# Keys of both heads split at once and placed by transfers, with single sets of tiles, in a hybrid attention block

## The chip, the cores and the metric

The kernel runs on one core of a Trainium2 chip. The core's engines are named as the profile names them: PE multiplies matrices (PEld is its weight load), DVE is the vector engine, ACT the scalar engine with its function tables, POOL is GpSimd, and SP only issues transfers. The metric is the device time of one execution in microseconds; for each kernel several executions are timed and their median is given.

## The reference

The input is a sequence of 512 tokens of width 1024, with 16 learned tokens put in front (528 positions). After a layer norm, one matrix of 1024 x 10240 projects every position to ten groups of 1024 channels: queries, keys, values and gates of two attentions, and two merge gates. Both attentions work in causal blocks of 128 queries, so query block i (0 to 3) sees 16 + 128 (i + 1) keys: 144, 272, 400, 528.

```python
def diff_attn_block(q, k, v, q_pos, slopes, lam):          # 8 heads, each with 2 maps of width 64
    s = einsum(q, k) * 64 ** -0.5 ;  s = where(dist >= 0, s - slope * dist, -inf)
    p = softmax(s)
    a = p[map 0] - lam * p[map 1]
    return a @ v                                           # then an RMS norm per head

def stick_breaking_block(q, k, v, q_pos):                  # 16 heads of width 64
    before = k_pos < q_pos                                 # strictly earlier keys
    z = einsum(q, k) * 64 ** -0.5
    log_keep = where(before, log_sigmoid(-z), 0)
    suffix = cumsum of log_keep over the later keys
    a = where(before, exp(log_sigmoid(z) + suffix), 0)
    return a @ v
```

Each attention's output is multiplied with the SiLU of its gate and projected by a 1024 x 1024 matrix; the two results are merged by sigmoid gates, projected once more, added to the residual and normalised.

## The kernel before

All matrix products are done at reduced-precision speed with corrected operands: an operand is split into a rounded high part (a cast on ACT) and the remainder (a subtraction on DVE), and a product is the sum of high x high, high x low and low x high. Weights come in halves of 128 x 512 (`fetch`, L127), are split by `hi` (L153, ACT) and `lo` (L158, DVE) four halves ahead of their use, with six buffers of raw weights.

The work in the middle is a list of 16 units: eight differential heads ("d") and then eight pairs of stick-breaking heads ("s"). While the attention of unit u is computed, PE also projects the keys and values of unit u + 1 and the queries of unit u + 2; in "s" units two gates besides. `proj_tok` (L450 to L452) makes 512-wide products, `proj_pos` (L466) 264-wide ones, two halves of the 528 positions each.

- `stage_k` (L540) takes the projected keys of a unit from PSUM. Partitions 0 to 63 hold map or head 0, partitions 64 to 127 hold map or head 1. For each of the two, a tile `K[c]` of 128 x 2 x 528 is filled: its own half of the partitions with the high part and the remainder, the other half with the high part again and zeros (the queries' remainder stands there, so one product over 128 rows gives two of the three terms). The copies go from PSUM directly, for each c and each half: a cast (L551), a subtraction (L552) and a second cast to the other partitions (L553). There are two sets of `K`, used in turn.
- `logits` (L597) computes the scores of one query block: two products into one PSUM tile (high and low part of the keys, L608), except for block 0, whose 2 x 144 columns fit in one product (L602); there the low part's scores stand beside the high part's and are added on DVE (`with_lo`, L615). Block 3 (528 keys) is done in two halves.
- `d_scores` (L673): per query block from 3 down to 0 and per map, DVE adds the bias and finds the row's extreme (L701), ACT takes the exponential with its sum (L705); then DVE takes reciprocals (L709), multiplies one with -lambda (L710), scales the first map (L711) and combines both maps into `apad` (L712). The exponentials stand in tiles e0 and e1, two sets each.
- `s_scores` (L754): per query block DVE adds a mask of -1e30 to the last 128 columns of the scores (L767), ACT takes two sigmoids (`om` of -z, L770, and `sg` of z, L772), DVE multiplies `om` cumulatively from the last key backwards (a scan with a minimum that changes nothing, L775) and then `sg` with the shifted result into `apad` (L776).
- `transposed` (L618) turns `apad` on PE and splits it; `values` (L566) turns and splits the values; the products with them follow (`d_values`, `s_values`).

What sets the order: the first part up to L811 and the last from L848 are held to the written order by `keep_order`. In the middle each engine's order is set at build time by a planner, which simulates the engines and takes, of the instructions that are ready, the one written first. `run` (L495) writes the work down: the projections are a sequence of pieces with a nominal length, and attention's steps are put between them at due times (for a "d" unit: the ten score steps from 0.0 every 0.85, the three transposes from 11.0, the values' product at 14.5, out of 15.7 nominal). SP's queue, with all weight loads, and the other queues run in the planned order; an instruction whose semaphore is not there holds up all behind it on its queue.

Of the kernel before, what the change touches and what calls it, by code (L numbers as in the profile page):

```python
# [20 lines left out]
M = 16  # L21
L = M + S
NB = S // P
H2 = L // 2
# [7 lines left out]
ZW = 1344  # L32
# [11 lines left out]
def hybrid_block_kernel(ctx: ExitStack, tc: tile.TileContext, x, meta, emb_g, emb_b, w_in, b_gate,  # L44
# [209 lines left out]

    neg = const.tile([P, M + P], F32, name="neg")
    g.memset(neg, 0.0)
    g.affine_select(neg, neg, pattern=[[-1, M + P]], compare_op=ALU.is_gt, fill=-1e30, base=M, channel_multiplier=1)
# [249 lines left out]
    with tc.tile_pool(name="att", bufs=1) as ap:  # L507
# [7 lines left out]
        tails = {}  # L515
        for n in ("d", 0, 1):
            tails[n] = (ap.tile([P, P], F32R, name=f"v4{n}"), ap.tile([P, 32], F32R, name=f"a4{n}"))
            for t in tails[n]:
                g.memset(t.bitcast(F32), 0.0)


        keys = [[ap.tile([P, 2, L], F32R, name=f"k{c}{n}") for c in range(2)] for n in range(2)]
        for n in range(2):
            for c, oth in ((0, HI), (1, LO)):
                g.memset(keys[n][c][oth, 1, :].bitcast(F32), 0.0)  # L525
# [14 lines left out]
        def stage_k(unit, kind, n):  # L540

            pss = []
            proj = proj_pos(pss, "k" + kind, n)
            K = keys[n % 2]
            for m in range(2):
                while len(pss) == m:
                    yield next(proj, 0.33)
                o = ts(m, H2)
                for c, own, oth in ((0, LO, HI), (1, HI, LO)):
                    ps = pss[m][own, :H2]  # L550
                    s.copy(K[c][own, 0, o], ps)  # L551
                    v.tensor_tensor(K[c][own, 1, o], ps, K[c][own, 0, o].bitcast(F32), op=ALU.subtract)  # L552
                    s.copy(K[c][oth, 0, o], ps)  # L553
            unit["K"] = K

# [10 lines left out]
        def values(unit, kind):  # L566

            vT = unit["vT"]
            tv = ptp.tile([P, 512], F32, tag="tp", name="tv")
            for j in range(4):  # L570
                pe.transpose(tv[:, ts(j, P)], vT[:, ts(j, P)], ident)  # L571
            tvv = tv.rearrange("p (j d) -> p j d", j=4)
            V = [ap.tile([P, 4, P], F32R, tag=f"v{c}", name=f"V{c}") for c in range(2)]
            t4 = ptp.tile([P, 512], F32, tag="tp", name="t4")[:M, :P]
            pe.transpose(t4, vT[:, 512:528], ident)
            if kind == "d":
                s.copy(V[0][:, :3, :], tvv[:, :3, :])
                v.tensor_tensor(V[1][:, :3, :], tvv[:, :3, :], V[0][:, :3, :].bitcast(F32), op=ALU.subtract)
                vf = ap.tile([P, P], F32, tag="vf", name="vf")
                s.copy(vf, tvv[:, 3, :])  # L580
                v4 = tails["d"][0]
                s.copy(v4[:M], t4)
                s.copy(v4[32:32 + M], t4)
                v.tensor_tensor(v4[64:64 + M], t4, v4[:M].bitcast(F32), op=ALU.subtract)
                unit["V"] = V, vf
            else:
                for c, own, oth in ((0, LO, HI), (1, HI, LO)):
                    src = tvv[:, :, own]
                    s.copy(V[c][:, :, own], src)
                    v.tensor_tensor(V[c][:, :, oth], src, V[c][:, :, own].bitcast(F32), op=ALU.subtract)  # L590
                    v4 = tails[c][0]
                    s.copy(v4[:M, own], t4[:, own])
                    s.copy(v4[32:32 + M, own], t4[:, own])
                    v.tensor_tensor(v4[:M, oth], t4[:, own], v4[:M, own].bitcast(F32), op=ALU.subtract)
                unit["V"] = V

        def logits(A, K, i):  # L597

            nk, q = NKEY[i], A[:, ts(i, P)]
            if 2 * nk <= 512:  # L600
                ps = psc.tile([P, 512], F32, tag="sc", name="sc")
                pe.matmul(ps[:, :2 * nk].rearrange("p (a n) -> p a n", a=2), q, K[:, :, :nk], start=True, stop=True)  # L602
                yield ps, 0, nk, ps[:, nk:2 * nk]
                return
            for k0, n in [(0, nk)] if nk <= 512 else [(0, H2), (H2, H2)]:
                ps = psc.tile([P, 512], F32, tag="sc", name="sc")
                for m in range(2):
                    pe.matmul(ps[:, :n], q, K[:, m, k0:k0 + n], start=(m == 0), stop=(m == 1))  # L608
                yield ps, k0, n, None

        def with_lo(lo, b, t):

            if lo is None:
                return b
            v.tensor_tensor(t, lo, b, op=ALU.add)  # L615
            return t
# [56 lines left out]
        def d_scores(unit, h):  # L673

            K = unit["K"]
# [11 lines left out]
            E = [ap.tile([P, ZW], F32, tag=f"e{c}", name=f"e{c}", bufs=2) for c in range(2)]  # L687
# [3 lines left out]
            for i in reversed(range(NB)):  # L691
                nk = NKEY[i]
                e = [E[c][:, ZOFF[i]:ZOFF[i] + nk] for c in range(2)]
                for c in range(2):
                    m = mn[:, i, c, :]
                    for n, (ps, k0, use, lo) in enumerate(logits(A[c], K[c], i)):
                        if n == 1:
                            yield
                        b0 = 384 - P * i + k0
                        t = with_lo(lo, bias[:, b0:b0 + use], e[c][:, k0:k0 + use])  # L700
                        v.tensor_tensor_reduce(e[c][:, k0:k0 + use], ps[:, :use], t, -1.0, 3e38, ALU.add, ALU.min,  # L701
                                               m[:, n:n + 1])
# [7 lines left out]
                v.tensor_scalar(r[:, 1:2], r[:, 1:2], nlam, None, op0=ALU.mult)  # L710
                v.tensor_scalar(e[0], e[0], r[:, 0:1], None, op0=ALU.mult)  # L711
# [42 lines left out]
        def s_scores(unit, c, first):  # L754
            K = unit["K"]
            A = unit["A"]
            a = apads[c]
            sg = ap.tile([P, ZW], F32, tag="e0", name="sgm", bufs=2)
            om = ap.tile([P, ZW], F32, tag="e1", name="om", bufs=2)
            for i in reversed(range(NB)):  # L760
                nk, z0 = NKEY[i], ZOFF[i]
                for n, (ps, k0, use, lo) in enumerate(logits(A[c], K[c], i)):
                    if n == 1:
                        yield
                    if k0 + use == nk:
                        w = P if lo is None else use
                        v.tensor_tensor(ps[:, use - w:use], ps[:, use - w:use], with_lo(lo, neg[:, M + P - w:], om[:, ds(z0, w)]),  # L767
                                        op=ALU.add)
# [36 lines left out]
        run([stage_k(units[0], *UNITS[0])], [(2.7, then)])  # L805
# [7 lines left out]
        for u, (kind, n) in enumerate(UNITS):  # L813
# [6 lines left out]
            pending = []  # L820
            if kind == "d":
# [256 lines left out]
```

## Time and profile before

| | before |
|---|---|
| median of 3 runs (range) | 732.13 us (731.3 to 732.39) |
| the profiled execution, its own time | 732.59 us |
| its span from first to last instruction | 730.8 us |
| mean granted clock of PE | 0.995 |
| busy: PE, DVE, ACT, POOL | 718.3, 580.3, 447.2, 89.9 us |
| bytes moved by transfers | 71.84 MB |

A page of the profile lists busy times, the chain of work that ended last, and groups of instructions by line with their shape, count, busy time and mean duration in ns, and the idle time of the engine before them. The waits view lists who waited for whom: total us, times, longest. A timeline row has start, duration (of the whole row, if several like instructions are merged), engine, line, operation, output and inputs, shape and count. A row of the windows view has a stretch, its length, and for PE, PEld, DVE, ACT and POOL the busy time with the count of rows, then the granted clock, the transfer engines' share and GB/s. Transfers have size and median time from issue to landing. Matmul durations overlap: one starts before the one ahead has ended.

### The profile page before, as it was taken

The numbers are of one execution on the slowest core, as the hardware profiler recorded it, in microseconds if no ns is written. First come the engines' busy times: TensorE is split into PE (matmuls) and PEld (weight loads), VectorE is DVE, ScalarE is ACT, GpSimd is POOL, SyncE is SP. The second block draws the span as 40 slices with busy tenths as digits, with TensorE's granted clock in tenths as the row PEclk, the third lists the DMA queues.
The fourth block names the chain that finished last, engine by engine and source line by source line (L and its number), as shares of the span: only waits on it lengthen the run. The fifth ranks groups of instructions, "written<-read, shape, count | busy, mean of one in ns | idle before, by whom it ended". The sixth has DMA issues, their size and how long they took to land.

```text
span 730.8 us, 13070 instructions
## 1 busy us (share of the span) xinstructions
PE 718.3 (98%) x4658; PEld 657.6 (90%) x4658; DVE 580.3 (79%) x1304; ACT 447.2 (61%) x1101; POOL 89.9 (12%) x116
## 2 busy tenths in 40 slices
PE   9999999999999999999999999999999999999994
PEld 8999999999999989898989898988888998999883
DVE  6888778878886699696969696969476888788887
ACT  5686677777877858575757574756355456555300
POOL 3211110011000000000000000001012202130002
PEclk9999999999999999999999999999999999999998
DMA  9142221222132221323132212222239837696902
GB/s 280 50 116 87 60 73 44 87 59 73 45 87 58 73 73 53 92 61 86 45 90 70 85 46 87 73 73 59 73 89 181 177 105 185 135 183 188 315 16 102
DMA packets 121347, 71.84 MB, mean 98 GB/s; under 512 B 4241, under 2 KB 114994, under 8 KB 121282
## 3 DMA queue, kind: packets, MB, share of 16 engines
q1 hardware_dynamic: 111650, 64.18, 30.0%
q0 software_dynamic: 9312, 5.77, 6.0%
q10 hardware_dynamic: 320, 1.06, 0.4%
q8 instruction: 37, 0.61, 0.3%
q14 instruction: 28, 0.23, 0.1%
HBM read 67.32 MB, written 2.10 MB: 95 GB/s over the span
## 4 chain that ended last, share of the span: by engine, by line
PE 89%; DVE 5%; DMA 3%; POOL 1%; ACT 1%; issue 1%; SPq 0%; POOLq 0%; DVEq 0%; ACTq 0%
PE ps L466 25%; PE ps L450 12%; PE ps L451 12%; PE ps L452 12%; PE q L886 10%; PE sc L608 5%; PE t L621 4%; DMA raw<-in_w_out_dram 2%; PE t L626 1%; PE bank L341 1%; PE av L789 1%; PE tv L571 1%; PE av L790 1%; DMA eb<-in_emb_ln_b_dram 1%; DVE hr L1035 1%
## 5 line engine op out<-in xcount | busy, mean ns | idle before, releaser
L158 DVE TENSOR_TENSOR wl<-raw,wh 128x512 fp32r<-128x512 f32 x180 | 124.3, 697 | 47.8 <-ACT wh L153 46.7
L466 PE MATMUL ps<-hTh,wh 128*128 128x264 f32 x512 | 147.4, 288 | 0.0
L466 PE MATMUL ps<-hTl,wh 128*128 128x264 f32 x512 | 146.3, 286 | 0.0
L466 PE MATMUL ps<-hTh,wl 128*128 128x264 f32 x512 | 145.8, 285 | 0.0
L452 PE MATMUL ps<-hTh,wl 128*128 128x512 f32 x368 | 144.8, 393 | 0.0
L450 PE MATMUL ps<-hTh,wh 128*128 128x512 f32 x368 | 144.7, 393 | 0.0
L451 PE MATMUL ps<-hTl,wh 128*128 128x512 f32 x368 | 144.5, 393 | 0.0
L153 ACT CAST wh<-raw 128x512 fp32r<-128x512 f32 x180 | 109.9, 621 | 49.8 <-PE ps L451 38.9
L466 PEld LDWEIGHTS ps<-hTh,wh 128*128 128x128 f32 x512 | 96.4, 188 | 1.2
L466 PEld LDWEIGHTS ps<-hTl,wh 128*128 128x128 f32 x512 | 96.4, 188 | 0.7
L466 PEld LDWEIGHTS ps<-hTh,wl 128*128 128x128 f32 x512 | 96.4, 188 | 0.3
L452 PEld LDWEIGHTS ps<-hTh,wl 128*128 128x128 f32 x368 | 69.2, 188 | 13.5
L451 PEld LDWEIGHTS ps<-hTl,wh 128*128 128x128 f32 x368 | 69.2, 188 | 12.9
L450 PEld LDWEIGHTS ps<-hTh,wh 128*128 128x128 f32 x368 | 69.2, 188 | 12.7
L886 PE MATMUL q<-gh,wh 128*128 128x256 f32 x224 | 63.5, 283 | 0.2 <-ACT t L895 0.2
L886 PE MATMUL q<-gh,wl 128*128 128x256 f32 x224 | 63.4, 283 | 0.0
L886 PE MATMUL q<-gl,wh 128*128 128x256 f32 x224 | 63.4, 283 | 0.0
L632 DVE TENSOR_TENSOR al<-t,ah 128x512 fp32r<-128x512 f32 (+2 forms) x88 | 45.7, 526 | 17.9 <-ACT ah L631 11.0
L775 DVE TENSOR_TENSOR_SCAN om<-om 128x528 f32<-128x528 f32 (+1 forms) x64 | 55.7, 877 | 5.1 <-ACT om L770 4.4
L608 PE MATMUL sc<-k,A 128*128 128x264 f32 (+2 forms) x256 | 56.4, 308 | 0.2 <-POOL k L525 0.2
L631 ACT CAST ah<-t 128x512 fp32r<-128x512 f32 (+2 forms) x88 | 40.0, 465 | 25.4 <-PE t L621 18.1
L770 ACT ACTIVATE om<-sc 128x264 f32<-128x264 f32 (+3 forms) x80 | 31.8, 397 | 20.0 <-DVE sc L767 17.7
(243 smaller groups left out, 1442.3 us busy)
## 6 DMA issues: line engine op xcount, KB each, us to landing
raw<-in_w_in_dram SPq DMA_DIRECT2D x152, 256.0 KB, 3.0
raw<-in_w_out_dram SPq DMA_DIRECT2D x16, 256.0 KB, 3.6
raw<-in_w_br_diff_dram SPq DMA_DIRECT2D x12, 256.0 KB, 4.3
raw<-in_w_br_sb_dram SPq DMA_DIRECT2D x12, 256.0 KB, 4.5
raw<-in_w_in_dram SPq DMA_DIRECT2D x4, 512.0 KB, 6.2
rawa<-in_w_br_diff_dram SPq DMA_DIRECT2D x8, 256.0 KB, 4.6
rawa<-in_w_br_diff_dram POOLq DMA_DIRECT2D x8, 256.0 KB, 5.9
rawa<-in_w_br_sb_dram SPq DMA_DIRECT2D x8, 256.0 KB, 4.1
```

The source lines that it names most:

```text
L153: s.copy(wh, raw)
L158: eng.tensor_tensor(wl, raw, wh.bitcast(F32), op=ALU.subtract)
L450: pe.matmul(ps, wh[:, k % 4, :], hTh[:, k, M:], start=(k == 0), stop=False)
L451: pe.matmul(ps, wh[:, k % 4, :], hTl[:, k, M:], start=False, stop=False)
L452: pe.matmul(ps, wl[:, k % 4, :], hTh[:, k, M:], start=False, stop=(k == KT - 1))
L466: pe.matmul(ps[:, :H2], a[:, k % 4, :], b[:, k, ts(c, H2)], start=(k == 0 and m == 0), stop=(k == KT - 1 and m == 2))
L608: pe.matmul(ps[:, :n], q, K[:, m, k0:k0 + n], start=(m == 0), stop=(m == 1))
L631: s.copy(h, t[:, o:o + w])
L632: v.tensor_tensor(l, t[:, o:o + w], h.bitcast(F32), op=ALU.subtract)
L770: s.activation(om[:, o], ps[:, :use], AF.Sigmoid, scale=-1.0)
L775: v.tensor_tensor_scan(rev, rev, rev, 1.0, ALU.mult, ALU.min)
L886: pe.matmul(bank, a[:, k, :], b[:, n, k, :], start=start and k == 0 and m == 0, stop=k == 3 and m == 2, skip_group_check=not start)
```

## The change

- Keys: `stage_k` now splits both heads at once. One cast and one subtraction over all 128 partitions write a staging tile `t` (two of them, one per half). A new function `store_k` copies from it into the four places of `K[0]` and `K[1]` by transfers on SP's queue, eight per unit. There is one set of `K`. `store_k` is put among the steps of the unit before at 9.2 nominal (10.6 in the first "s" unit). Unit 0 keeps the direct copies (`direct=True`).
- Scores: the form of block 0 with both parts in one product goes; block 0 is done like blocks 1 and 2, with two products into the same columns. `with_lo` goes.
- Exponentials: one set of e0 and e1 (`E`) for all units, and the two sigmoids of `s_scores` stand in them too.
- Mask: the tile `neg` and the addition to the scores go. The scan's second input is a tile `after` (1 at masked keys, 0 elsewhere) with a maximum, so that it stays at 1 through the masked keys; GpSimd sets the masked part of `sg` to zero.
- First map: its scaling and the product of the reciprocal with -lambda move from DVE to GpSimd.
- Values of the "s" units: the copies for both heads are done by one instruction each, through strided views of one tile `V`, and likewise for the last 16 positions (`v4s`).

```diff
-    neg = const.tile([P, M + P], F32, name="neg")
-    g.memset(neg, 0.0)
-    g.affine_select(neg, neg, pattern=[[-1, M + P]], compare_op=ALU.is_gt, fill=-1e30, base=M, channel_multiplier=1)
...
+        v4d = ap.tile([P, P], F32R, name="v4d")
+        v4s = ap.tile([P, 4, 64], F32R, name="v4s")
...
+        E = [ap.tile([P, ZW], F32, name=f"e{c}") for c in range(2)]
+        after, staged = [], []
...
-        keys = [[ap.tile([P, 2, L], F32R, name=f"k{c}{n}") for c in range(2)] for n in range(2)]
-        for n in range(2):
-            for c, oth in ((0, HI), (1, LO)):
-                g.memset(keys[n][c][oth, 1, :].bitcast(F32), 0.0)
+        K = [ap.tile([P, 2, L], F32R, name=f"k{c}") for c in range(2)]
+        for c, own, oth in HEADS:
+            g.memset(K[c][oth, 1, :].bitcast(F32), 0.0)
...
-        def stage_k(unit, kind, n):
+        def stage_k(unit, kind, n, direct=False):
...
-                o = ts(m, H2)
-                for c, own, oth in ((0, LO, HI), (1, HI, LO)):
-                    ps = pss[m][own, :H2]
-                    s.copy(K[c][own, 0, o], ps)
-                    v.tensor_tensor(K[c][own, 1, o], ps, K[c][own, 0, o].bitcast(F32), op=ALU.subtract)
-                    s.copy(K[c][oth, 0, o], ps)
-            unit["K"] = K
+                o, ps = ts(m, H2), pss[m][:, :H2]
+                if direct:
...
+                t = ap.tile([P, 2, H2], F32R, tag="ks", name="ks", bufs=2)
+                s.copy(t[:, 0], ps)
+                v.tensor_tensor(t[:, 1], ps, t[:, 0].bitcast(F32), op=ALU.subtract)
+                staged.append((o, t))
+
+        def store_k():
+
+            for o, t in staged:
+                for c, own, oth in HEADS:
+                    nc.sync.dma_start(K[c][own, :, o].bitcast(F32), t[own].bitcast(F32))
+                    nc.sync.dma_start(K[c][oth, 0, o].bitcast(F32), t[own, 0].bitcast(F32))
+            staged.clear()
...
-                for c, own, oth in ((0, LO, HI), (1, HI, LO)):
-                    src = tvv[:, :, own]
-                    s.copy(V[c][:, :, own], src)
-                    v.tensor_tensor(V[c][:, :, oth], src, V[c][:, :, own].bitcast(F32), op=ALU.subtract)
...
+                for h, l, src in ((V[:, :, 0:4:3], V[:, :, 1:3], tvv.rearrange("p j (c d) -> p j c d", c=2)),
+                                  (v4s[:M, 0:4:3], v4s[:M, 1:3], t4.rearrange("p (c d) -> p c d", c=2))):
+                    s.copy(h, src)
+                    v.tensor_tensor(l, src, h.bitcast(F32), op=ALU.subtract)
...
-            if 2 * nk <= 512:
-                ps = psc.tile([P, 512], F32, tag="sc", name="sc")
-                pe.matmul(ps[:, :2 * nk].rearrange("p (a n) -> p a n", a=2), q, K[:, :, :nk], start=True, stop=True)
-                yield ps, 0, nk, ps[:, nk:2 * nk]
-                return
...
-            E = [ap.tile([P, ZW], F32, tag=f"e{c}", name=f"e{c}", bufs=2) for c in range(2)]
...
-                v.tensor_scalar(r[:, 1:2], r[:, 1:2], nlam, None, op0=ALU.mult)
-                v.tensor_scalar(e[0], e[0], r[:, 0:1], None, op0=ALU.mult)
+                g.tensor_scalar(e[0], e[0], r[:, 0:1], None, op0=ALU.mult)
+                g.tensor_tensor(r[:, 1:2], r[:, 1:2], nlam, op=ALU.mult)
...
-            sg = ap.tile([P, ZW], F32, tag="e0", name="sgm", bufs=2)
-            om = ap.tile([P, ZW], F32, tag="e1", name="om", bufs=2)
+            sg, om = E
...
-                    if k0 + use == nk:
-                        w = P if lo is None else use
-                        v.tensor_tensor(ps[:, use - w:use], ps[:, use - w:use], with_lo(lo, neg[:, M + P - w:], om[:, ds(z0, w)]),
-                                        op=ALU.add)
...
+                own = sg[:, ds(z0 + nk - P, P)]
+                g.affine_select(own, own, pattern=[[-1, P]], compare_op=ALU.is_gt, fill=0.0, base=0, channel_multiplier=1)
                 rev = om[:, z0:z0 + nk][:, ::-1]
-                v.tensor_tensor_scan(rev, rev, rev, 1.0, ALU.mult, ALU.min)
+                v.tensor_tensor_scan(rev, rev, after[0][:, L - nk:][:, ::-1], 1.0, ALU.mult, ALU.max)
...
-        run([stage_k(units[0], *UNITS[0])], [(2.7, then)])
+        run([stage_k(units[0], *UNITS[0], True)], [(2.7, then)])
...
+            if not last:
+                steps.append((10.6 if kind == 's' and n == 0 else 9.2, store_k))
...
+                    after.append(ap.tile([P, L], F32, tag="bias", name="after", bufs=2))
+                    g.memset(after[0], 0.0)
+                    own = after[0][:, L - P:]
+                    g.affine_select(own, own, pattern=[[-1, P]], compare_op=ALU.is_gt, fill=1.0, base=0, channel_multiplier=1)
```

More of the change, by code (lines that the diff above doesn't have):

```diff
@@ L515, in hybrid_block_kernel @@
         tails = {}
+        v4d = ap.tile([P, P], F32R, name="v4d")
+        v4s = ap.tile([P, 4, 64], F32R, name="v4s")
         for n in ("d", 0, 1):
-            tails[n] = (ap.tile([P, P], F32R, name=f"v4{n}"), ap.tile([P, 32], F32R, name=f"a4{n}"))
-            for t in tails[n]:
-                g.memset(t.bitcast(F32), 0.0)
-        keys = [[ap.tile([P, 2, L], F32R, name=f"k{c}{n}") for c in range(2)] for n in range(2)]
-        for n in range(2):
-            for c, oth in ((0, HI), (1, LO)):
-                g.memset(keys[n][c][oth, 1, :].bitcast(F32), 0.0)
+            tails[n] = (v4d if n == "d" else v4s[:, 2 * n:2 * n + 2].rearrange("p c d -> p (c d)"),
+                        ap.tile([P, 32], F32R, name=f"a4{n}"))
+        for t in (v4d, v4s, *(tails[n][1] for n in tails)):
+            g.memset(t.bitcast(F32), 0.0)
+        E = [ap.tile([P, ZW], F32, name=f"e{c}") for c in range(2)]
[3 more added lines that the diff above has]
+            g.memset(K[c][oth, 1, :].bitcast(F32), 0.0)
         def stage_q(unit, kind, n):
@@ L572, in values @@
             tvv = tv.rearrange("p (j d) -> p j d", j=4)
-            V = [ap.tile([P, 4, P], F32R, tag=f"v{c}", name=f"V{c}") for c in range(2)]
+            V = ap.tile([P, 1024], F32R, tag="v", name="V")
             t4 = ptp.tile([P, 512], F32, tag="tp", name="t4")[:M, :P]
@@ L576, in values @@
             if kind == "d":
+                V = V.rearrange("p (c j d) -> p c j d", c=2, j=4)
+                V = [V[:, c] for c in range(2)]
                 s.copy(V[0][:, :3, :], tvv[:, :3, :])
@@ L586, in values @@
             else:
-                for c, own, oth in ((0, LO, HI), (1, HI, LO)):
-                    src = tvv[:, :, own]
-                    s.copy(V[c][:, :, own], src)
-                    v.tensor_tensor(V[c][:, :, oth], src, V[c][:, :, own].bitcast(F32), op=ALU.subtract)
[L591 to L595, printed above, removed]
+                V = V.rearrange("p (j c d) -> p j c d", j=4, c=4)
+                for h, l, src in ((V[:, :, 0:4:3], V[:, :, 1:3], tvv.rearrange("p j (c d) -> p j c d", c=2)),
+                                  (v4s[:M, 0:4:3], v4s[:M, 1:3], t4.rearrange("p (c d) -> p c d", c=2))):
+                    s.copy(h, src)
+                    v.tensor_tensor(l, src, h.bitcast(F32), op=ALU.subtract)
+                s.copy(v4s[32:32 + M, 0:4:3], t4.rearrange("p (c d) -> p c d", c=2))
+                unit["V"] = [V[:, :, 2 * c:2 * c + 2].rearrange("p j c d -> p j (c d)") for c in range(2)]
         def logits(A, K, i):
             nk, q = NKEY[i], A[:, ts(i, P)]
-            if 2 * nk <= 512:
-                ps = psc.tile([P, 512], F32, tag="sc", name="sc")
-                pe.matmul(ps[:, :2 * nk].rearrange("p (a n) -> p a n", a=2), q, K[:, :, :nk], start=True, stop=True)
-                yield ps, 0, nk, ps[:, nk:2 * nk]
-                return
             for k0, n in [(0, nk)] if nk <= 512 else [(0, H2), (H2, H2)]:
@@ L608, in logits @@
                     pe.matmul(ps[:, :n], q, K[:, m, k0:k0 + n], start=(m == 0), stop=(m == 1))
[L609 to L616, printed above, removed]
+                yield ps, k0, n
         def transposed(ta, a, head):
@@ L673, in d_scores @@
         def d_scores(unit, h):
-            K = unit["K"]
             A = unit["A"]
@@ L695, in d_scores @@
                     m = mn[:, i, c, :]
-                    for n, (ps, k0, use, lo) in enumerate(logits(A[c], K[c], i)):
+                    for n, (ps, k0, use) in enumerate(logits(A[c], K[c], i)):
                         if n == 1:
```

14 lines of the change are left out of this document (8 added, 6 removed).

## The prediction, made before the changed kernel ran

> **What bounds the kernel now.** I read the page first: busy time and the chain that ended last.
>
> ```profile
> span 730.8 us, 13070 instructions
> PE 718.3 (98%) x4658; PEld 657.6 (90%) x4658; DVE 580.3 (79%) x1304; ACT 447.2 (61%) x1101; POOL 89.9 (12%) x116
> PE 89%; DVE 5%; DMA 3%; POOL 1%; ACT 1%; issue 1%; SPq 0%; POOLq 0%; DVEq 0%; ACTq 0%
> ```
>
> PE is busy 98% of the span and holds 89% of the chain. A busy PE may still be a badly fed one, so the second view is what PE waited for, and the third its share between the first scores of one head and of the next, and in one pair of stick-breaking heads.
>
> ```profile
> PE sc L608 <- POOL k L525: 0.2, 1, 0.2
> PE q L886 <- ACT t L895: 0.2, 1, 0.2
> ...
> 132.21:156.42 24.21, 24.21 (x174) 22.90 (x172) 20.62 (x60) 18.33 (x49) 3.23 (x2) 1.00 0.23 67
> 156.42:180.62 24.20, 24.20 (x174) 22.87 (x172) 19.40 (x60) 18.26 (x49) 3.12 (x2) 1.00 0.20 58
> ...
> 415.00:452.00 37.00, 37.00 (x238) 33.59 (x237) 29.76 (x61) 23.29 (x62) 2.58 (x2) 1.00 0.25 72
> ```
>
> After its warm-up PE waits 0.4 us in all. In both kinds of unit (24.2 us per differential head, 37.0 us per stick-breaking pair) it is busy throughout at the full granted clock, while DVE is busy 19.4 to 20.6 of 24.2 us and 29.8 of 37. Work taken from DVE and ACT therefore buys nothing here; work added to PE is paid in full. The question that decides is what the change adds to PE, and PE's own durations overlap, so I take prices from the spacing of starts in the timeline.
>
> ```profile
> 296.54 0.39 PE L452 MATMUL ps<-hTh,wl 128*128 128x512 f32 x1
> 296.77 0.24 PE L789 MATMUL av<-ah,V 128*128 128x160 f32 x1
> 296.84 0.43 PE L450 MATMUL ps<-hTh,wh 128*128 128x512 f32 x1
> 297.11 0.40 PE L451 MATMUL ps<-hTl,wh 128*128 128x512 f32 x1
> ...
> 173.31 0.29 PE L602 MATMUL sc<-k,A 128*128 128x288 f32 x1
> 173.44 0.28 PE L466 MATMUL ps<-hTh,wh 128*128 128x264 f32 x1
> ...
> 156.54 0.27 PE L621 MATMUL t<-idents,apad 128*128 128x128 f32 x1
> 156.54 0.60 PE L621 MATMUL t<-idents,apad 128*128 128x128 f32 x4
> ...
> L602 PE MATMUL sc<-k,A 128*128 128x288 f32 x32 | 9.7, 304 | 0.0
> ```
>
> A 512-wide product takes 0.23 us (296.54 to 296.77). A 160-wide one seems to take 0.07, but the 512 behind it then takes 0.27: the pair costs 0.34, so the narrow one costs 0.34 - 0.23 = 0.11. One 128-wide transpose lasts 0.27 and four in a row span 0.60 (two answers on the same stretch), so they start (0.60 - 0.27) / 3 = 0.11 apart. A product narrower than 264 columns thus has a floor near 0.11 us. The 288-wide score product of query block 0 costs 0.13 (173.31 to 173.44).
>
> **The change part by part.** *Scores of query block 0 (L600 to L604).* One product over both parts of the keys, 288 wide, becomes two of 144, each with its own weight load (the page counts 4658 of either). 32 products (the L602 row: 16 units, 2 maps) become 64. By the floor: 2 x 0.11 to 0.12 - 0.13 = 0.09 to 0.11, times 32 = 2.9 to 3.5 us. If only the visible spacing counted (0.07): 2 x 0.07 - 0.13 = 0.01, times 32 = 0.3 us. I take 0.115: 0.10 x 32 = 3.2 us, since the floor shows twice, in a transpose and in a narrow product.
>
> The Trainium skill ("TensorE: Matmul & The Clock Gate", section Back-to-back issue gap) gives about 81 ns per product for a stream of weight loads and products at 128 columns; taken as it stands for 144 columns, that is an estimate of 2 x 0.081 - 0.13 = 0.03, or 1.0 us over 32 pairs. The 0.11 us of this trace at 128 and 160 columns speaks against it, and the measurement decides.
>
> *Work that leaves DVE and ACT.*
>
> ```profile
> L552 DVE TENSOR_TENSOR k<-ps,k 64x264 fp32r<-64x264 f32 x64 | 27.3, 427 | 8.2 <-ACT k L551 7.3
> L553 ACT CAST k<-ps 64x264 fp32r<-64x264 f32 x64 | 24.0, 374 | 15.1 <-DVE k L552 14.2
> L563 ACT COPY vT<-ps 128x264 f32<-128x264 f32 x32 | 12.2, 381 | 0.3
> L767 DVE TENSOR_TENSOR sc<-sc,neg 128x128 f32<-128x128 f32 x48 | 13.7, 289 | 1.9 <-PE sc L608 1.3
> L767 DVE TENSOR_TENSOR sc<-sc,om 128x144 f32<-128x144 f32 x16 | 4.9, 308 | 0.3
> L615 DVE TENSOR_TENSOR e<-sc,bias 128x144 f32<-128x144 f32 x16 | 4.8, 301 | 0.1
> L710 DVE TENSOR_SCALAR rz<-rz,nlam 128x1 f32<-128x1 f32 x32 | 6.8, 211 | 0.8
> L711 DVE TENSOR_SCALAR e<-e,rz 128x528 f32<-128x528 f32 x8 | 3.9, 485 | 0.0
> L711 DVE TENSOR_SCALAR e<-e,rz 128x272 f32<-128x272 f32 x8 | 2.9, 362 | 0.0
> ```
>
> Partitions do not set a duration (64x264 takes 374 ns on ACT, 128x264 takes 381), so both heads at once halve it. Keys: DVE 4 x 0.427 to 2, saving 0.85 us a unit; ACT eight of 0.374 to two of 0.381, saving 2.2. A differential head also loses L710 (4 x 0.211), L711 (0.485, 0.362 and two between or just below: about 1.55) and L615 (2 x 0.301): DVE saves 3.8 us of some 20. A stick-breaking pair loses the mask (6 x 0.289 + 2 x 0.308) and its two L615 forms (0.6): with the keys 3.8 us of 29.8; the merged copies of values save a few tenths more. In all about 60 us of DVE and 35 of ACT, priced at nothing: they lie beside a PE that never waits. At most the 0.2 us of L608 could return.
>
> *Work that goes to POOL.*
>
> ```profile
> L684 POOL TENSOR_SCALAR bias<-bias 128x528 f32<-128x528 f32 x8 | 14.1, 1758 | 21.8 <-DVE e L615 21.6
> L257 POOL TENSOR_SCALAR_AFFINE_SELECT neg<-neg 128x144 f32<-128x144 f32 x1 | 0.3, 298 | 0.0
> 148.60 1.40 POOL L735 TENSOR_TENSOR sql<-sq,sqh 128x512 fp32r<-128x512 f32 x1 [18.32 <-ACT sqh L734]
> 148.88 1.42 DVE L712 SCALAR_TENSOR_TENSOR apad<-e,rz,e 128x272 f32<-128x272 f32 x1
> 152.71 0.37 DVE L712 SCALAR_TENSOR_TENSOR apad<-e,rz,e 128x144 f32<-128x144 f32 x1
> ```
>
> Scaling the first map is the operation of L684: 1.76 us for 528 columns, by width 1.33, 0.91 and 0.48 for the others, 4.5 us a head, plus four tiny products. L712 now queues on DVE behind that. The last one of this head ends at 153.1 and its first transposes start at 156.54: 3.4 us of cover, against 0.48 us for the last block, or 1.4 with the block before still running. Without cover it would be about 1 us a head, 8 us. The selection on the sigmoid (8 a pair, about 0.3 us each) runs beside the scan over the other tile. DVE and POOL do disturb each other: L712 took 1.42 us beside L735. The Trainium skill ("SBUF — State Buffer", section Who interferes with whom) calls this an exclusive lock between a DVE instruction with two SBUF inputs and a GpSimd one that reads SBUF; the row agrees. Even if all 4.5 us fell on DVE, a head's DVE would be at 20.6 - 3.8 + 4.5 = 21.3 of 24.2: still under PE.
>
> *Keys by transfers, one set.*
>
> ```profile
> 174.63 0.29 PE L602 MATMUL sc<-k,A 128*128 128x288 f32 x1
> 180.62 0.65 PE L608 MATMUL sc<-k,A 128*128 128x264 f32 x4
> 175.16 0.37 SPq L127 DMA_DIRECT2D raw<-in_w_in_dram  x1
> raw<-in_w_in_dram SPq DMA_DIRECT2D x152, 256.0 KB, 3.0
> out_dram<-hr SPq DMA_DIRECT2D x8, 256.0 KB, 2.0
> ```
>
> Eight transfers a unit, 120 in all, of at most 132 KB, are queued on SP among the weight loads. They wait for the last scores (ended 174.9 here), because the one set is still read until then; the next scores start at 180.62, 5.7 us later. Eight issues of 0.37 are 3.0 us, and landing takes 2.0 to 3.0 (a transfer between two tiles is not in this trace): the last lands 5.0 to 6.0 us after the last scores. The first scores need only one map's four, the second map's follow them. So it is hidden, barely. Weight loads queued behind wait up to 3 us more, with six buffers ahead: nothing. In stick-breaking units the gates stand between and the window is wider.
>
> *First unit.*
>
> ```profile
> 32.85 0.28 PE L608 MATMUL sc<-k,A 128*128 128x264 f32 x1
> 33.34 0.39 PE L608 MATMUL sc<-k,A 128*128 128x264 f32 x1 [0.20 <-POOL k L525]
> ```
>
> Here PE waits for POOL clearing the keys; half of that clearing goes: 0 to -0.4 us, I take -0.2.
>
> **The sum.** 3.2 - 0.2 = +3.0 us on PE's chain. The profiled execution took 732.59 us (span 730.8 and 1.8 around it), 0.46 above the median of 732.13; so 735.6 for such an execution, 735.1 against the median.
>
> **The rivals.** *A, narrow products are cheap (ends on the other side):* two adjacent products on the same weights might run at the visible 0.07 us spacing, the debt being paid only once. For it: the 0.07 itself. Against: the 0.27 behind it, and each 144 has its own load. It decides where the pair costs below 0.18 us; price +0.3 - 0.2: 732.2, no change. *B, the relief returns time:* a lighter DVE lets the planner place PE's work better. For it: DVE ends late behind the projections, so scores are spread out. Against: two equal heads take 24.21 and 24.20 us, both wholly busy. Removing all the 0.4 us of waits beside rival A gives 731.9; to be faster than noise it needs some 1.5 us that no row shows: 730.4. *C, keys come late:* if the scores stand ahead of the landing, or one load (0.37) sits among the eight, the last lands at 174.9 + 6.0 + 0.4 = 181.3, 0.7 late, at eight boundaries between differential heads and into the first pairs: +5.6 us, 740.7. For it: the 5.7 us window. Against: half the transfers suffice to start, and the planner has projections to put in between. It decides when landing exceeds the window.
>
> **How the numbers follow.** Forecast 0.52; A 0.15; B 0.16, of which 0.09 faster; C 0.17. Below 0.2% (1.5 us, about what a measurement tells from no change) counts as the same. Slower: 0.52 + 0.17 = 0.69; same 0.15 + 0.07 = 0.22; faster 0.09. The forecast's own range is 734.5 to 735.8. The range 732.0 to 739.5 takes in A, most of B and the milder half of C, and leaves out under 2 in 10.
>
> **What the new profile would show.** Right: the L602 form is gone, 64 products of 144 columns stand in its place, pair spacing near 0.22 us; PE still about 98% with no wait on the keys; DVE near 520 us, ACT near 410, POOL near 150; heads 24.4 instead of 24.2 us apart. Wrong: pair spacing near 0.14 (A); PE's waits naming a transfer into the keys (C); a shorter distance between heads with PE's count up (B). A first transpose that waits for the probabilities would break the cover given to POOL.

## The result and the profile after

| | before | changed |
|---|---|---|
| median (range), 5 runs each | 732.13 us (731.26 to 732.39) | 736.03 us (734.92 to 737.56) |
| ratio, 95% interval | | 1.006 (1.0044 to 1.0077) |
| the profiled execution, its own time | 732.59 us | 734.92 us |
| its span | 730.8 us | 733.1 us |
| bytes moved by transfers | 71.84 MB | 84.03 MB |

The changed kernel is slower, by 3.9 us in the medians; the forecast was +3.0 us, 735.1. The two profiled executions differ by 2.3 us, in time and in span alike. First the page of the changed kernel: its span, its busy times, its chain by engine, and two of its transfer groups (count, size, median us from issue to landing).

```profile
span 733.1 us, 13328 instructions
PE 719.2 (98%) x4690; PEld 659.4 (90%) x4690; DVE 529.9 (72%) x1098; ACT 411.1 (56%) x987; POOL 176.6 (24%) x241
PE 88%; DVE 6%; DMA 3%; POOL 1%; issue 1%; ACT 1%; SPq 0%; POOLq 0%; ACTq 0%; DVEq 0%
...
k<-ks SPq DMA_DIRECT2D x60, 132.0 KB, 2.6
k<-ks SPq DMA_DIRECT2D x60, 66.0 KB, 2.0
```

PE has 32 products more (4690 instead of 4658) and is still what the chain runs along. DVE lost 50 us and ACT 36; POOL gained 87. The second view is what PE waited for.

```profile
PE q L886 <- ACT t L895: 0.2, 1, 0.2
PE sc L615 <- POOL k L525: 0.2, 1, 0.2
```

Both waits are those of before, and no transfer into the keys is among them. Third, the windows. I cut the span at the first projection product of unit 1's keys and at the first product of the gated projections behind the units; between them lies **the middle**: all sixteen units but the very start, and the merge gates' projections right behind them. The rows give stretch, length, busy us (with count) of PE, PEld, DVE, ACT and POOL, granted clock, transfer share and GB/s. The kernel before:

```profile
39.57:562.17 522.60, 522.60 (x3358) 476.63 (x3357) 415.88 (x986) 352.63 (x906) 49.37 (x42) 1.00 0.28 76
```

The changed kernel, its middle and one differential head:

```profile
39.70:564.24 524.54, 524.54 (x3389) 479.51 (x3387) 365.04 (x780) 316.33 (x791) 137.59 (x172) 1.00 0.37 99
156.64:181.00 24.36, 24.36 (x175) 23.08 (x173) 16.51 (x47) 16.06 (x43) 9.11 (x10) 1.00 0.37 98
```

PE is busy for the whole of the middle in both, at the full granted clock. The middle grew by 1.94 us and the head by 0.16 (24.20 before). By the starts of the same products in the traces, all kernels of this text come apart like this (us):

| kernel | start | middle | gated projections, first half | second half | output product | tail |
|---|---|---|---|---|---|---|
| before | 39.57 | **522.60** | 67.54 | 46.10 | 44.13 | 10.87 |
| changed | 39.70 | **524.54** | 67.54 | 46.10 | 44.08 | 11.19 |
| changed, again | 40.32 | **524.56** | 67.54 | 46.67 | 44.13 | 10.16 |
| e1, one product again | 39.77 | **521.38** | 67.54 | 46.10 | 44.09 | 9.93 |
| e1, again | 39.81 | **521.35** | 67.54 | 46.09 | 44.14 | 11.34 |
| e2, before with two products | 39.86 | **525.83** | 67.54 | 46.81 | 44.08 | 10.39 |
| e3, before with the keys' transfers | 39.57 | **522.06** | 67.54 | 47.93 | 44.08 | 10.56 |
| e3, again | 40.56 | **522.07** | 67.54 | 46.10 | 44.10 | 10.27 |
| e4, before with 32 products of 32 columns | 39.79 | **527.09** | 67.54 | 46.20 | 44.08 | 10.56 |
| e7, the same of 128 columns | 39.82 | **527.11** | 67.54 | 46.26 | 44.13 | 10.63 |
| e8, the same of 256 columns | 39.68 | **527.28** | 67.54 | 48.49 | 44.10 | 10.35 |
| e9, 32 columns, light weights | 39.78 | **527.02** | 67.54 | 46.10 | 44.08 | 10.61 |
| e5, e1 with the scaling on DVE | 40.35 | **521.73** | 67.54 | 46.10 | 44.13 | 9.93 |
| e6, e1 with direct keys | 40.27 | **522.81** | 67.54 | 46.10 | 44.08 | 10.36 |

In the three kernels of which two executions were traced, the middle repeats to 0.03 us. The start (39.6 to 40.6), the second half of the gated projections (46.1 to 48.5) and the tail (9.9 to 11.3) change from one execution to the next. So the cost of an edit to the units is read from the middle. The medians can differ by more: those of the changed kernel stand 3.9 and 3.0 us above the kernel before, of which the middle holds 1.94.

### The profile page after: what moved, and what is told of

Read it like the earlier page. It is cut to its first block, busy times and chain, and to the rows that moved or that the text cites. A ratio compares the mean times of both kernels' runs of the same rounds, so it can differ in the third digit from the quotient of the medians.

```text
span 733.1 us, 13328 instructions
## 1 busy us (share of the span) xinstructions
PE 719.2 (98%) x4690; PEld 659.4 (90%) x4690; DVE 529.9 (72%) x1098; ACT 411.1 (56%) x987; POOL 176.6 (24%) x241
## 2 busy tenths in 40 slices
DMA packets 134788, 84.03 MB, mean 115 GB/s; under 512 B 6161, under 2 KB 128434, under 8 KB 134722
## 4 chain that ended last, share of the span: by engine, by line
PE 88%; DVE 6%; DMA 3%; POOL 1%; issue 1%; ACT 1%; SPq 0%; POOLq 0%; ACTq 0%; DVEq 0%
PE ps L462 25%; PE ps L448 12%; PE ps L446 11%; PE ps L447 11%; PE q L886 10%; PE sc L615 6%; PE t L621 4%; PE t L626 1%; DMA lgb<-in_ln_b_dram 1%; PE bank L337 1%; PE av L783 1%; PE tv L582 1%; PE av L784 1%; DVE hr L1035 1%; DMA raw<-in_w_out_dram 1%
## 5 line engine op out<-in xcount | busy, mean ns | idle before, releaser
L615 PE MATMUL sc<-k,A 128*128 128x264 f32 (+3 forms) x320 | 68.5, 298 | 0.2 <-POOL k L525 0.2
L769 DVE TENSOR_TENSOR_SCAN e<-e,after 128x528 f32<-128x528 f32 (+1 forms) x64 | 55.9, 883 | 13.2 <-ACT e L761 12.8
L767 POOL TENSOR_SCALAR_AFFINE_SELECT e<-e 128x128 f32<-128x128 f32 x64 | 38.7, 612 | 103.3 <-ACT e L763 94.6
L707 POOL TENSOR_SCALAR e<-e,rz 128x528 f32<-128x528 f32 (+3 forms) x32 | 38.4, 1200 | 100.2 <-DVE rz L706 100.2
```

The source lines that it names most:

```text
L707: g.tensor_scalar(e[0], e[0], r[:, 0:1], None, op0=ALU.mult)
L767: g.affine_select(own, own, pattern=[[-1, P]], compare_op=ALU.is_gt, fill=0.0, base=0, channel_multiplier=1)
L769: v.tensor_tensor_scan(rev, rev, after[0][:, L - nk:][:, ::-1], 1.0, ALU.mult, ALU.max)
```

## The experiments

**The changed kernel again**, beside a further set of runs of the kernel before; no edit.

> The changed kernel once more, for its spread (734.9 to 737.6 us in five executions, where the kernel before has 731.3 to 732.4) and a second trace. Theory of the narrow products (block 0's two products of 144 columns cost 0.2 us where one of 288 cost 0.13, nothing else on PE): 734.5 to 735.5 us, distance between the starts of two differential heads 24.36 us again, and what varies lies in the first 27 us or in the last 60. Rival of the late keys: PE waits for a transfer into the keys at some of the boundaries, which shows as single distances above 24.5 us, and the median stays near 736.

Measured: 735.16 us (734.79 to 737.02, 5 runs) against 732.15 (21 runs), ratio 1.0048 (1.0034 to 1.0061). Its middle:

```profile
40.32:564.88 524.56, 524.56 (x3389) 479.54 (x3387) 365.03 (x780) 316.60 (x791) 137.91 (x172) 1.00 0.37 99
```

The kernel is slower by 2.5 to 4.5 us, and the middle repeats. The sign of late keys, single distances above 24.5 us, shows once: the last differential head starts 25.34 us behind the one before it, in both traces. It isn't the keys: their last transfer there is issued at 199.1 us in the first trace, the scores start at 206.71, and PE reports no wait. e1 below, with the same transfers, has 24.13 at that place.

**e1, block 0 in one product again**, all else of the change kept. The second part of block 0's scores, which stands beside the first in PSUM, is added on DVE.

```diff
             nk, q = NKEY[i], A[:, ts(i, P)]
+            if 2 * nk <= 512:
+                ps = psc.tile([P, 512], F32, tag="sc", name="sc")
+                pe.matmul(ps[:, :2 * nk].rearrange("p (a n) -> p a n", a=2), q, K[:, :, :nk], start=True, stop=True)
+                yield ps, 0, nk, ps[:, nk:2 * nk]
+                return
...
+                        if lo is not None:
+                            v.tensor_tensor(e[c][:, k0:k0 + use], lo, t, op=ALU.add)
+                            t = e[c][:, k0:k0 + use]
...
+                    if lo is not None:
+                        v.tensor_copy(om[:, o], lo)
+                        v.tensor_tensor(ps[:, :use], ps[:, :use], om[:, o], op=ALU.add)
```

> The changed kernel with one edit taken back: the scores of query block 0 are again one product of 2 x 144 columns, and DVE adds the two parts (a copy and an addition per pair block in the stick-breaking units, one addition in the differential heads). Theory of the narrow products: back to 731.5 to 732.7 us, distance between differential heads 24.2 us. Rival of the late keys: stays at 735 to 736, since keys still come by transfers. If both count, about 733.5.

Measured: 731.2 us (730.44 to 733.05, 11 runs) against 732.15, ratio 0.9993 (0.9984 to 1.0002).

```profile
39.77:561.15 521.38, 521.38 (x3356) 476.35 (x3355) 380.39 (x828) 318.41 (x791) 130.85 (x172) 1.00 0.37 100
```

The split of block 0 costs 524.54 - 521.38 = 3.16 us of the middle, although DVE is 15 us less busy with it. What is left of the change is 521.38 - 522.60 = -1.22 us, which the expectation did not foresee (731.5 at the least, 731.2 measured).

**e2, the split alone**: the kernel before, with only the branch for block 0 removed.

```diff
-            if 2 * nk <= 512:
-                ps = psc.tile([P, 512], F32, tag="sc", name="sc")
-                pe.matmul(ps[:, :2 * nk].rearrange("p (a n) -> p a n", a=2), q, K[:, :, :nk], start=True, stop=True)
-                yield ps, 0, nk, ps[:, nk:2 * nk]
-                return
```

> The kernel before with that one edit alone: block 0's scores as two products of 144 columns into the same columns (the added DVE addition per block goes with it). Theory of the narrow products: +2.1 us by the changed kernel's trace (32 pairs x 0.065) to +3.2 by the prediction: 734.2 to 735.4. Rival of the late keys: within 0.5 us of the kernel before.

Measured: 736.75 us (736.33 to 738.07, 5 runs), ratio 1.0065 (1.0053 to 1.0078).

```profile
39.86:565.69 525.83, 525.79 (x3390) 480.00 (x3389) 405.84 (x954) 354.15 (x906) 51.07 (x42) 1.00 0.27 76
```

The middle is 3.23 us longer than before. The time is above the 735.4 expected at most; the second half of the gated projections, 0.7 us longer in this execution, is a part of that. Done alone and undone alone, the edit has the same price, 0.10 us for each of 32. The changed kernel's timeline of PE shows where it sits (start, duration of the row, line, shape, count):

```profile
172.09 0.28 PE L462 MATMUL ps<-hTh,wh 128*128 128x264 f32 x1
172.21 0.34 PE L615 MATMUL sc<-k,A 128*128 128x144 f32 x2
172.39 0.33 PE L462 MATMUL ps<-hTl,wh 128*128 128x264 f32 x1
172.55 0.28 PE L462 MATMUL ps<-hTh,wl 128*128 128x264 f32 x1
```

From the pair's start to the next product pass 0.18 us, but that product holds PE for 0.16 instead of its usual 0.12 (172.09 to 172.21): the pair costs 0.34 - 0.12 = 0.22, against 0.13 of the single 288.

**e3, the transfers alone**: the kernel before, with both heads' keys split at once, `store_k`, and one set of keys.

```diff
-        keys = [[ap.tile([P, 2, L], F32R, name=f"k{c}{n}") for c in range(2)] for n in range(2)]
+        K = [ap.tile([P, 2, L], F32R, name=f"k{c}") for c in range(2)]
...
+                t = ap.tile([P, 2, H2], F32R, tag="ks", name="ks", bufs=2)
+                s.copy(t[:, 0], ps)
+                v.tensor_tensor(t[:, 1], ps, t[:, 0].bitcast(F32), op=ALU.subtract)
+                staged.append((o, t))
...
+            if not last:
+                steps.append((10.6 if kind == 's' and n == 0 else 9.2, store_k))
```

> The kernel before with the other edit alone: the keys of both heads split at once, placed by transfers on SP's queue, one set of keys. Theory of the narrow products: within 0.5 us of the kernel before, 731.6 to 732.6. Rival of the late keys: +1.5 to +5 us, with PE's waits naming the keys and a wider spread of the executions.

Measured: 733.51 us (731.66 to 735.27, 11 runs), ratio 1.0019 (1.0009 to 1.0028). The middle, then the second half of the gated projections:

```profile
39.57:561.63 522.06, 522.06 (x3356) 476.47 (x3355) 397.62 (x956) 321.53 (x815) 49.78 (x42) 1.00 0.38 100
629.17:677.10 47.93, 46.17 (x360) 44.80 (x359) 37.17 (x71) 25.31 (x51) 10.50 (x10) 1.00 0.74 165
```

The waits of PE in the same execution:

```profile
PE q L897 <- ACT t L902: 1.0, 1, 1.0
PE q L897 <- ACT t L906: 0.7, 1, 0.7
```

The time is outside the 0.5 us that were expected, but no wait of PE names the keys' transfers. In the part that was edited the kernel is 0.54 us shorter; what made this execution longer lies over 190 us behind the last key transfer (issued at 475 us): at 668.9 and 672.8 us PE waits 1.7 us in all for ACT's copies out of PSUM. Whether that belongs to this kernel was open.

**e3 again**, one more execution.

> The kernel before with the keys by transfers, one more look for its trace. Theory that the differences outside the middle belong to single executions: the middle is 522.1 us again (within 0.05), while the output projections (46.1 to 47.9 us in the second half) and the last 10 to 11 us differ. Rival that they belong to the kernel: the second half of the output projections takes 47.9 us again.

Measured: one execution of 732.43 us. The same two stretches:

```profile
40.56:562.63 522.07, 522.07 (x3357) 476.46 (x3356) 397.73 (x956) 321.20 (x815) 49.69 (x42) 1.00 0.38 100
630.17:676.26 46.09, 45.89 (x360) 44.73 (x359) 37.16 (x71) 25.42 (x51) 10.47 (x10) 1.00 0.78 172
```

The stall is gone and the middle is the same, so it is not fixed to the kernel; but one execution can't say whether it comes as often here as before, and the median of e3 stays 1.4 us above that of before. This stall is a possible reason; it is not shown to be the reason.

**e5, the scaling back on DVE**, within e1: the first map's scaling and the product with -lambda.

```diff
-                g.tensor_scalar(e[0], e[0], r[:, 0:1], None, op0=ALU.mult)
-                g.tensor_tensor(r[:, 1:2], r[:, 1:2], nlam, op=ALU.mult)
+                v.tensor_scalar(r[:, 1:2], r[:, 1:2], nlam, None, op0=ALU.mult)
+                v.tensor_scalar(e[0], e[0], r[:, 0:1], None, op0=ALU.mult)
```

> The changed kernel with block 0's scores in one product again, and in addition the first map's scaling and the product with -lambda back on DVE. Theory that work moved off DVE is worth nothing while PE never waits: the middle stays at 521.4 us (within 0.2) and the time at 731.2 (within 0.6). Rival that the relief of DVE is what took 1.2 us off the middle: it returns in part, +0.3 to +0.8 us. Rival that the long way over GpSimd costs time: the middle gets shorter by 0.2 us or more.

Measured: 731.9 us (731.12 to 732.21, 11 runs) against 732.42 (21 runs), ratio 0.999 (0.9982 to 0.9999).

```profile
40.35:562.08 521.73, 521.73 (x3357) 476.53 (x3355) 389.78 (x892) 318.93 (x791) 89.49 (x108) 1.00 0.38 100
```

The middle is 0.35 us longer than in e1: outside the 0.2 of the first theory, inside the +0.3 to +0.8 of the rival. So the scaling on GpSimd is worth 0.35 us, in the direction of a gain; it is no cost.

**e6, direct keys**, within e1: two sets of keys and the copies of before.

```diff
+        keys = [[ap.tile([P, 2, L], F32R, name=f"k{c}{n}") for c in range(2)] for n in range(2)]
...
+            K = unit["K"] = keys[n % 2]
...
-            return [stage_k(unit, kind, n), stage_v(unit, kind, n)]
+            return [stage_k(unit, kind, n, True), stage_v(unit, kind, n)]
```

> The changed kernel with block 0's scores in one product again, and in addition the keys copied directly from PSUM for each head into two sets, as in the kernel before (no transfers). Theory that the single instructions for both heads, with the transfers, took the 0.5 us that the transfers' run alone took off the middle: the middle grows from 521.4 to 521.9 us. Rival that the transfers cost something hidden by other gains: the middle shrinks below 521.2.

Measured: 732.03 us (730.98 to 733.73, 11 runs) against 732.42, ratio 0.9997 (0.9987 to 1.0007).

```profile
40.27:563.08 522.81, 522.81 (x3359) 476.73 (x3357) 392.49 (x858) 350.03 (x882) 139.47 (x172) 1.00 0.28 76
```

Without the keys' part of the change nothing of the -1.22 us is left (522.81 against 522.60 before), where a loss of 0.5 us was expected. The parts of the change don't add up: the keys' part is worth 0.54 us in the kernel before and 1.43 in e1.

**e4, e7, e8: what a further narrow product costs.** The kernel before, with one product of 32, 128 or 256 columns ahead of each of the 32 products of block 0; its result is overwritten by the product behind it.

```diff
                 ps = psc.tile([P, 512], F32, tag="sc", name="sc")
+                pe.matmul(ps[:, :32], q, K[:, 0, :32], start=True, stop=True)
```

> The kernel before with one product of 32 columns put ahead of each of block 0's 32 score products, into columns that the next product overwrites (the result is unchanged). Theory of the floor (a product costs about 0.11 us however narrow): the middle, from the first keys' product of unit 1 to the first product of the output stage, grows by 32 x 0.10 to 0.12 = 3.2 to 3.8 us, the time to 735.3 to 736. Rival of streaming (columns at full clock plus about 13 ns): 32 x 0.03 = 0.8 us, 732.9.

Measured, 32 columns: 737.94 us (737.07 to 738.98, 4 runs) against 732.42, ratio 1.0077 (1.0063 to 1.009). Its middle, the one wait that PE reports in it, and PE's timeline around one such product:

```profile
39.79:566.88 527.09, 526.41 (x3391) 480.40 (x3390) 413.47 (x986) 355.12 (x906) 51.18 (x42) 1.00 0.27 75
...
PE ms L743 <- POOL sql L736: 0.5, 1, 0.5
...
318.80 0.18 PE L602 MATMUL sc<-k,A 128*128 128x32 f32 x1
318.83 0.38 PE L603 MATMUL sc<-k,A 128*128 128x288 f32 x1
319.05 0.28 PE L466 MATMUL ps<-hTh,wh 128*128 128x264 f32 x1
```

> As the run with the 32 extra products of 32 columns, but 128 columns wide. The 32-column run made the middle 4.5 us longer (0.14 us a product). Theory of a floor per product, however narrow: the same, 4.2 to 4.8 us. Rival of streaming: 96 columns more at 2.4 columns per ns are 0.04 us a product, +1.3 us, so 5.8 us.

Measured, 128 columns: one execution of 737.27 us, the kernel before beside it 731.81.

```profile
318.87 0.22 PE L602 MATMUL sc<-k,A 128*128 128x128 f32 x1
318.94 0.35 PE L603 MATMUL sc<-k,A 128*128 128x288 f32 x1
319.12 0.28 PE L466 MATMUL ps<-hTh,wh 128*128 128x264 f32 x1
```

> The same with 256 columns, where the kernel's own 264-wide products start 0.12 us apart. Theory of the floor: just above it, 4.4 to 5.2 us longer in the middle than the kernel before. Rival of streaming: 224 columns more than the 32-column run, 0.093 us a product, 3.0 us more: 7.5 us.

Measured, 256 columns: one execution of 739.22 us, 2.4 us of which are a longer second half of the gated projections (48.49).

```profile
318.83 0.28 PE L602 MATMUL sc<-k,A 128*128 128x256 f32 x1
318.94 0.30 PE L603 MATMUL sc<-k,A 128*128 128x288 f32 x1
319.08 0.28 PE L466 MATMUL ps<-hTh,wh 128*128 128x264 f32 x1
```

The three kernels lengthen the middle by 4.49, 4.51 and 4.68 us (527.09, 527.11 and 527.28 less 522.60), 0.14 to 0.15 us a product, whatever the width; 4.49 is above the 3.2 to 3.8 that 32 products at the floor were expected to cost. In each of them 0.67 to 0.68 us of this are no product: PE stands idle near 249 us (busy 526.41 of 527.09 with 32 columns), the most of it waiting for a subtraction on POOL (the L743 row), where the kernel before has no idle time. Without it the middles grow by 3.81, 3.83 and 4.01 us, 0.12 us a product. From the extra product's start to the one behind the pair pass 0.25 us in each timeline (318.80 to 319.05, 318.87 to 319.12, 318.83 to 319.08); a 288 alone takes 0.13. So up to 256 columns a product costs 0.12 us in the timeline: a narrow one starts its successor early (0.03 us behind it at 32 columns), and the successor holds PE for what was left (0.22 us). This is the floor that the prediction used, and the middle agrees with it.

**e9, the same with light weights**: 32 columns, and only 32 columns of weights.

```diff
+                pe.matmul(ps[:32, :32], q[:, :32], K[:, 0, :32], start=True, stop=True)
```

> As the 32-column run, but the extra product also takes only 32 of the 128 stationary columns, so its weight load is a quarter as wide. If the floor of 0.11 us is the load of 128 stationary columns: the extra cost falls to about a half or less, 1 to 2.3 us in the middle. If it is a fixed price per product: 4.5 us again.

Measured: one execution of 736.91 us.

```profile
318.71 0.18 PE L602 MATMUL sc<-k,A 128*32 128x32 f32 x1
318.73 0.38 PE L603 MATMUL sc<-k,A 128*128 128x288 f32 x1
318.95 0.29 PE L466 MATMUL ps<-hTh,wh 128*128 128x264 f32 x1
```

The pair takes 0.24 us, and the middle is 4.42 us longer than before, 3.74 without the same idle time of 0.68: the narrow product's own weight load does not set its price. The load of the product behind it has 128 columns in all four kernels. The Trainium skill ("TensorE: Matmul & The Clock Gate", section LDWEIGHTS (loading the stationary operand)) gives a load's time as its columns divided by 1.2 in ns, 107 for 128 columns, which is near the 0.12 us here. The profile's own rows for loads are longer, 188 ns for 128 columns (L603) and 108 for 32 (L602), and overlap; only their difference, 80 ns for 96 columns, fits that rate. That the successor's load is what PE waits for would agree with all four kernels, but no run took that load away, so it stays a guess beside a fixed price per product.

**e1 again**, since it is the one that could beat both.

> The changed kernel with block 0's scores in one product, timed once more against the kernel before, since its first interval (0.9984 to 1.0002) just reaches no change. Theory that its middle is 1.2 us shorter in every execution (521.4 against 522.6) and the rest is the same: 731.0 to 731.6 us, ratio 0.998 to 0.9995, middle 521.4 again. Rival that the shorter middle of one trace doesn't carry over to the time: ratio within 0.0005 of 1.

Measured: 731.4 us (730.82 to 732.16, 11 runs) against 732.41 (14 runs), ratio 0.9988 (0.9979 to 0.9997), with a middle of 521.35. The change without the split of block 0 is faster than the kernel before by some 0.9 us: with its first comparison (0.9993, an interval that reaches 1.0002) the sign is likely and the size at the edge of what these runs tell. It is faster than the changed kernel by 3.8 us in the medians of the repeats (735.16 and 731.4).

## Why the prediction was right, and where not

The time was right (736.03 and 735.16 for 735.1), and so was the step that decides. The sum was not made up as forecast, and that the medians came so near it is partly luck.

**Scores of block 0: right, in size too.** Forecast 0.10 x 32 = 3.2 us; measured 3.16 (undone) and 3.23 (alone). Rival A, narrow products at their visible spacing, fell: at 0.3 us for 32 pairs neither e1 nor e2 could have moved like that, and e4 shows why the visible spacing of 0.03 us is no price. The estimate of 1.0 us by the Trainium skill ("TensorE: Matmul & The Clock Gate", section Back-to-back issue gap) fell with it.

**Work that leaves DVE and ACT, "priced at nothing": wrong.** This is the step that failed. PE reports no wait in the middle before or after, yet the rest of the change takes 1.22 us from it, so the middle came out at +1.94 instead of +3.2 (the -0.2 of the first unit lies ahead of it). It is rival B in part, and smaller than the 1.5 us it had to bring. e6 shows that the gain needs the keys' part; e3 alone gives 0.54. What mechanism returns it is not settled.

Two things changed at once. The planner set PE's products in another order: it differs between the kernel before, the changed one, e1, e2, e3, e5 and e6. And the stream became denser. Compared only where a product has the same kinds of product in front and behind (output tile and width; 511 to 513 us of each middle), the distances between starts sum to 0.8 to 1.0 us less in e1 than before, 0.5 to 0.6 less in e5, 0.1 to 0.3 less in e3, and 0.1 more in e6. So most of the 1.22 is the same products closer together, and most of e3's 0.54 can be the order alone. How dense it is goes along with the busy times of DVE and ACT (e1 380 and 318 us, e5 390 and 319, e3 398 and 322, e6 392 and 350), but the kernels differ in more than these, so that is no cause shown.

The Trainium skill ("SBUF — State Buffer", section Who interferes with whom) says of the memory's ports that "PE and ACT never wait on anyone"; no run shows PE waiting there, and whether it is PSUM or the semaphores between the engines that cost the time in the kernel before, none tells.

**The sum against the median: partly luck.** The prediction set 735.6 for the profiled execution and 0.46 less for the median, as before. The profiled execution came at 734.92, 0.7 below: the middle fell 1.26 short of 3.2, since the relief had not been priced, and start, output product and tail together came out 0.4 longer where 0.2 less was forecast. The median stands 1.1 above that execution (in the repeat both are 735.16): start, second half of the gated projections and tail differ from one execution to the next. In the repeat the two errors cancel; in the first runs 0.9 us is left, which no trace places.

**Work that goes to POOL: right that it is hidden, wrong in its size.** The groups of the changed kernel (count, then busy us and mean ns of one):

```profile
L767 POOL TENSOR_SCALAR_AFFINE_SELECT e<-e 128x128 f32<-128x128 f32 x64 | 38.7, 612 | 103.3 <-ACT e L763 94.6 <-ACT a L649 8.7
L707 POOL TENSOR_SCALAR e<-e,rz 128x528 f32<-128x528 f32 x8 | 12.8, 1605 | 87.7 <-DVE rz L706 87.7
L707 POOL TENSOR_SCALAR e<-e,rz 128x400 f32<-128x400 f32 x8 | 12.5, 1556 | 8.3 <-DVE rz L706 8.3
L707 POOL TENSOR_SCALAR e<-e,rz 128x144 f32<-128x144 f32 x8 | 5.1, 640 | 3.2 <-DVE rz L706 3.1
L708 POOL TENSOR_TENSOR rz<-rz,nlam 128x1 f32<-128x1 f32 x32 | 7.7, 240 | 0.0
```

The selection takes 612 ns and not the 298 taken from L257, which adds 64 x 0.31 = 20 us. The scalings take 38.4 us over the four widths (32 x 1200 ns), 4.8 a head for 4.5, and the tiny products, named and not priced, 7.7. So POOL is at 176.6 us for a forecast near 150. The cover is seen in one head, on DVE and PE:

```profile
173.52 0.34 PE L615 MATMUL sc<-k,A 128*128 128x144 f32 x2
...
177.25 0.37 DVE L709 SCALAR_TENSOR_TENSOR apad<-e,rz,e 128x144 f32<-128x144 f32 x1
...
181.37 0.41 PE L615 MATMUL sc<-k,A 128*128 128x264 f32 x2
181.61 0.60 PE L621 MATMUL t<-idents,apad 128*128 128x128 f32 x4
```

The last combination ends at 177.6, and its first transpose starts at 181.61: 4.0 us of cover, where 3.4 less 0.5 to 1.4 for the scaling, 2.0 to 2.9, were forecast. DVE came out at 529.9 for a forecast near 520, ACT at 411.1 for 410. The durations of DVE's rows did fall by 60.7 us in all, as forecast; its busy time fell by 50.4, since it counts overlapping rows once.

**Keys by transfers, "hidden, barely": hidden with room.** Rival C fell. SP's queue at the same boundary:

```profile
169.40 0.47 SPq L564 DMA_DIRECT2D k<-ks  x1
...
173.04 0.62 SPq L563 DMA_DIRECT2D k<-ks  x1
173.77 0.53 SPq L564 DMA_DIRECT2D k<-ks  x1
174.40 0.62 SPq L563 DMA_DIRECT2D k<-ks  x1
175.68 0.37 SPq L127 DMA_DIRECT2D raw<-in_w_in_dram  x1
```

An issue takes 0.5 to 0.6 us and not 0.37, but the eight do not wait for the head's very last scores (173.52 above): the first is issued at 169.40, and the last at 174.40. With the group's 2.6 us it lands near 177.0, and the next scores start at 181.37. The forecast put all eight issues behind the last scores, which was the part of the step that was off; the landing, 2.0 to 3.0 us forecast, was right.

**First unit, -0.2: did not come.** PE's wait for the clearing of the keys is 0.2 us as before, though half of the clearing is gone; why was not followed up.

**Rows foreseen.** Heads 24.4 us apart (24.36), pairs near 0.22 us (0.22), PE at 98% without a wait on the keys: these came.

**Two slips in its own figures.** Rival B's 731.9 should read 732.0 (732.13 + 0.3 - 0.4). And the range from 732.0 does not take in "most of B": B's faster part, 0.09 of its 0.16, goes down to 730.4 and lies outside.

## What to carry to other kernels

On a PE that never waits, count products before columns: here every product of up to 256 columns cost the same 0.12 us, so one of 288 beats two of 144 by 0.10 us. Read such a price from the product behind the pair, since the narrow product's own distance to the next hides it. And price an edit on the stretch of the trace that it touches: the middle repeated to 0.03 us where whole executions of one kernel differed by 2 us and more.

## What the runs showed of the hardware that was not expected

- The width of a narrow product hardly mattered: 3.81, 3.83 and 4.01 us for 32 products of 32, 128 and 256 columns, and 3.74 with a quarter of the weights' columns (each without one idle stretch of PE of 0.67 to 0.68 us).
- A PE with no reported wait and no idle time ran its stream denser in the kernel in which DVE and ACT had less to do: middle 522.60 to 521.38 us, with DVE at 380 instead of 416 us and ACT at 318 instead of 353; 0.8 to 1.0 us of it between the same neighbours. What makes it denser is open.
- A selection on 128 x 128 took GpSimd 612 ns in the attention, a like one on 128 x 144 298 ns in the kernel before's beginning. And the scaling took 1556 ns for 400 columns against 1605 for 528, so it does not go by width alone. What slows them was not tried.
- The second half of the gated projections took 46.1 to 46.3 us in ten of fourteen executions and 46.7 to 48.5 in four; in e3 PE waited there 1.7 us for ACT's copies out of PSUM, in its second execution 0.2.
